# Longer transfer times, pinned first readers and a wider mark around solves in a hand-planned hybrid decoder layer

## The chip, the core and the metric

The kernel runs on one core of one Trainium2 chip. The metric is device microseconds (us) of one execution, taken as the median of several. TensorE (PE) multiplies matrices, with weight loads (PEld) running ahead of the matmuls; VectorE (DVE), ScalarE (ACT) and GpSimd (POOL) do the elementwise work; SyncE (SP) issues nearly all transfers (DMA). In this trace each engine, and the queue of SP, works through its instructions in the order of its program; one that has to wait holds those behind it.

## What is computed

One decoder layer on 2048 tokens of width 1024, all in float32. A normalised input is multiplied by one wide matrix whose columns feed three groups of heads and a gate. The parts that matter here:

```python
h = rms_norm(x, norm_in[l])
c_q, c_kv, k_rope, gdn_qkv, gdn_a, gdn_b, mem_q, gate = split_cols(h @ w_in[l], IN_SPLITS)
...
o_mla = causal_mla(q_nope, q_rope, k_nope, k_rope, v_mla).reshape(B, S, MLA_HEADS * MLA_V)
qkv = jax.nn.silu(causal_depthwise_conv(gdn_qkv, gdn_conv[l])).astype(jnp.float32)
...
L = jnp.where(strict, jnp.einsum('bhncd,bhnjd->bhncj', k_beta, k) * decay, 0.0)
T = lax.linalg.triangular_solve(L + eye, jnp.broadcast_to(eye, L.shape), left_side=True,
                                lower=True, unit_diagonal=True)
...
o_mem = memory_attention(mem_q..., mk..., mv...)
mixed = jnp.concatenate([o_mla, o_gdn, o_mem], axis=-1) * jax.nn.silu(gate)
x = x + mixed @ w_out[l]
return rms_norm(x, norm_final)
```

The second group of heads (gated delta rule, "GDN") needs a triangular solve for every chunk of tokens.

## The kernel before, in words

**Products in three parts.** Every large product is made of three matmuls on a high and a low part of each operand (`mm3`): high by high, high by low, low by high. So each weight tile `wr` that is loaded from HBM is split before use: `wh` is a rounded copy made on ACT or DVE, `wl` is the rest `wr - wh`, made on POOL or DVE. `lesser` (L618 to L620) picks the engine for `wl` (and for `bwl`, the same thing for the smaller weights `bw`): POOL, if the planner's clock of POOL isn't ahead of its clock of PE by more than a slack (500 ns for `wl`, 0 for `bwl`), else DVE.

**Two phases.** Phase 1 (up to about 1150 us; `phase[0] == 0`) streams the input projection: for each half of the tokens 34 column tiles, each in two units of 24 products (matmuls named `ip`). While these run, background generators do everything that hangs on their results: convolutions, the low-rank projections (`qb`, `kb`, `vb`), the memory keys and values (`mk`, `mv`, weights `bw`), and for each half and each of four heads one GDN chain (`delta_head`, eight chains in all). Phase 2 is attention (`sc`, `pt`, `av`) and the output projection (`op`).

**One GDN chain.** Row factors go out to memory and come back spread over all partitions (stores `rows_n`, `rows_g`, loads `fr`, `gr`). DVE scales keys and queries by them (`kq`), PE multiplies (`kk`), DVE writes the triangular systems `LT`; their diagonal blocks go out (`lsys`) and come back in another layout (`lt`). Then comes **the solve**: 62 small GpSimd instructions in a row that alternate between `pr` and `X` (L937 to L943). The result is stored (`tsys<-X`) and loaded into the tile `inv` (`inv0`, `inv1`); DVE transposes blocks of it (`mid<-inv`), PE finishes the inverse, and a scan over eight chunks follows (`pa`, `st`, `st_odd`), with loads of `gv` and `aT`.

**The order is planned by a model.** The Python program keeps a clock `T` for each engine and one for the transfers, with a cost for every instruction (`Timed`, L245 to L258). The clock of PE advances with the matmuls of the stream. A background generator is resumed when the clock of PE has reached the time at which, by the model, its last step is done (`pump`); at that moment its next instructions are written into the program. So the model's idea of when a transfer lands or a solve ends decides where the dependent instructions stand in the queues of DVE, ACT, POOL, PE and SP. For a transfer (`issue`, L292 to L303) the model takes 475 ns of SP, then

```python
        t = max(t + 650, T["DMA"]) + free(out) * out.shape[0] * 4 / 360
        T["DMA"] = t
        wrote(out, "SP", t + 700)
```

so the transfers run one after the other at 360 bytes per ns, and a reader on another engine sees the tile 900 ns after that (700 and 200). A transfer whose source isn't ready yet is kept in a list (`late`) with a similar estimate. For a solve the model takes 147 ns and 2.1 ns an element for each instruction, and about 100 ns between them.

**After the planner, a list scheduler.** The program so written passes through a scheduler that may move an instruction ahead of earlier ones of its engine where its own estimate says that it can start sooner; `tc.keep_in_program_order` forbids that for one instruction: it stays behind the instruction traced just before it on its engine. The stores `tsys<-X` and the loads of `inv` are already held that way (`behind=True`), as are transfers into `rows*` and `lsys*`.

Of the kernel before, what the change touches and what calls it, by code (L numbers as in the profile page):

```python
# [39 lines left out]
TRIG_AT = 1  # L40
MEM_AT = 44
STRICT = False
LONG = "012k3q", "0123qk"
CONV = 4
CBIAS = 2000.0
# [4 lines left out]
SLACK = {"wl": 500.0, "bwl": 0.0}  # L50
# [16 lines left out]
def hybrid_layer(ctx, tc, a, out):  # L67
    nc = tc.nc
    V, A, G, PE = nc.vector, nc.scalar, nc.gpsimd, nc.tensor
# [80 lines left out]
    PS = {"mm": 4, "g": 2, "scan": 2}  # L150
    rings = {t: [] for t in PS}
    in_psum = set()
    tiles = set()
    step_end = [0.0]
    tab = [None]

    def free(ap):
        return int(np.prod(ap.shape[1:]))
# [77 lines left out]
    pin = [False]  # L236
    phase = [0]

    def pinned(ins):

        if pin[0]:
            tc.keep_in_program_order(ins)
        return ins

    class Timed:  # L245
# [3 lines left out]
        def __getattr__(self, op):  # L249
            f = getattr(self.eng, op)  # L250

            def call(*args, **kw):
                out = kw["out"] if "out" in kw else args[0]
                outs = [out] + ([kw["accum_out"]] if "accum_out" in kw else [])
                ins = [x for x in (*args, *kw.values()) if hasattr(x, "tensor") and not any(x is o for o in outs)]
                note(self.name, self.cost(op, args, kw, out), outs, ins)
                return pinned(f(*args, **kw))  # L257
            return call  # L258

    V, A, G, PE = (Timed(nc.vector, "DVE", dve_cost), Timed(nc.scalar, "ACT", act_cost),  # L260
# [6 lines left out]
    def dma(out, in_, awaited=True, first=False, behind=False):  # L267
        touch(in_, out)
        t = max(arrival(in_, "SP"), used.get(out.tensor.name, 0.0), floor.get(out.tensor.name, 0.0))
        crowd = not first and T["PE"] > 0 and T["SP"] > T["PE"] + BACK  # L270
        if crowd or t > max(0.0, max(T["PE"], T["SP"]) + DEFER):
            if crowd:
                t = max(t, T["SP"] + 475 * sum(x[0] >= T["SP"] for x in late))
            late.append((t, out, in_, behind))
            t += 1125 + free(out) * out.shape[0] * 4 / 360
            wrote(out, "SP", t + 700)
            if awaited:
                step_end[0] = max(step_end[0], t + 900)
        else:
            issue(t, out, in_, behind, awaited)  # L280
# [9 lines left out]
        pinned(nc.gpsimd.dma_start(out=raw(out), in_=raw(in_)))  # L290

    def issue(t, out, in_, behind, awaited):  # L292
        t = max(T["SP"], T["PE"], t) + 475
        T["SP"] = t
        t = max(t + 650, T["DMA"]) + free(out) * out.shape[0] * 4 / 360
        T["DMA"] = t
        wrote(out, "SP", t + 700)
        used[in_.tensor.name] = max(used.get(in_.tensor.name, 0.0), t + 200)
        if awaited:
            step_end[0] = max(step_end[0], t + 900)  # L300
        ins = pinned(nc.sync.dma_start(out=raw(out), in_=raw(in_)))  # L301
        if (behind or out.tensor.name[:4] in ('rows','lsys')) and not pin[0]:
            tc.keep_in_program_order(ins)  # L303
# [313 lines left out]

    def lesser(name):  # L618

        return G if T["POOL"] <= T["PE"] + SLACK[name] else V  # L620

    class Job:

# [210 lines left out]
    def delta_head(hf, h, q, k, res):  # L834
# [102 lines left out]
        for j in range(31):  # L937
            n = j // 4 + 1
            w = 31 - j
            prv = pr[:, 0:n * w].rearrange("p (n w) -> p n w", w=w)  # L940
            G.tensor_tensor(prv, X[:, 0:n, j:j + 1].broadcast_to([P, n, w]),
                            lt[:, j, j + 1:32].unsqueeze(1).broadcast_to([P, n, w]), op=ALU.mult)
            G.tensor_tensor(X[:, 0:n, j + 1:32], X[:, 0:n, j + 1:32], prv, op=ALU.subtract)  # L943
        yield 0
        for cs in range(4):
            dma(out=tsys[hf][h].rearrange("s (n e) i -> e s n i", e=4)[cs], in_=X[cs * 32:(cs + 1) * 32],
# [1234 lines left out]
```

## Time and profile before

| what | value |
|---|---|
| median of 3 runs | 1859.41 us (1857.65 to 1865.71) |
| the profiled execution | 1856.66 us, span of its instructions 1854.9 us |
| PE busy | 1745.2 us, 94% of the span |
| DVE, ACT, POOL busy | 1203.0, 733.1, 510.2 us |
| mean granted TensorE clock | 0.978 of full |

Busy time counts the engine's own work; a waiting engine is idle. Nearly all instructions carry the line of the helper that records them (L257) and transfers that of `issue` (L301), so groups are told apart by their tiles: `out<-in`, buffer numbers left out. `PEclk` is the granted clock of TensorE, 1 being 2.4 GHz and 0.5 being 1.2 GHz; a value between them is a mean of stretches at either level. "SPq" is SP's queue of transfers.

### The profile page before, as it was taken

How to read it: one execution, taken by the hardware profiler on the slowest of the kernel's cores; microseconds unless marked ns; L12 is line 12 of the kernel's file. 1: busy time of each engine (PE TensorE's matmuls, PEld its weight loads, DVE VectorE, ACT ScalarE, POOL GpSimd, SP SyncE). 2: the span in 40 equal slices, each digit the busy share in tenths (PEclk: the TensorE clock that was granted, in tenths of full speed). 3: DMA queues.
4: the chain of work that ended last, by engine and by line, in shares of the span. 5: the costliest groups of instructions: out<-in, count | busy, mean ns of one | idle time of the engine just before them, and what ended most of it. 6: DMA issues, size and time to landing. Idle time of an engine off the chain costs nothing.

```text
span 1854.9 us, 28648 instructions
## 1 busy us (share of the span) xinstructions
PE 1745.2 (94%) x9780; PEld 1464.9 (79%) x9780; DVE 1203.0 (65%) x2696; ACT 733.1 (40%) x1792; POOL 510.2 (28%) x834
## 2 busy tenths in 40 slices
PE   6898799989998999899999799999999999899998
PEld 5676678877776888687888687889999998788886
DVE  8878586657776777546668263777776777543443
ACT  6354234334343445223454233455555556222221
POOL 5524615241161223342212524001111103511120
PEclk8899899999999999999999899999999999999999
DMA  5445347524647543455555367626252535754541
GB/s 191 156 127 153 118 154 219 183 82 136 213 131 242 160 158 121 151 195 165 181 190 192 99 208 225 183 89 185 73 173 70 157 105 176 228 168 157 184 150 61
DMA packets 242481, 292.49 MB, mean 158 GB/s; under 512 B 46848, under 2 KB 148224, under 8 KB 242336
## 3 DMA queue, kind: packets, MB, share of 16 engines
q1 hardware_dynamic: 239264, 282.28, 48.8%
q0 software_dynamic: 3072, 8.39, 1.3%
q8 instruction: 77, 1.26, 0.3%
q14 instruction: 68, 0.56, 0.1%
HBM read 197.53 MB, written 93.06 MB: 157 GB/s over the span
## 4 chain that ended last, share of the span: by engine, by line
PE 56%; DMA 6%; DVE 4%; POOL 3%; issue 2%; ACT 1%; SPq 1%; DVEq 0%; POOLq 0%; ACTq 0%
PE ip L257 14%; PE op L257 14%; PE sc L257 9%; PE av L257 6%; PE pt L257 4%; PE qb L257 2%; PE pa L257 2%; POOL X L257 1%; POOL pr L257 1%; SPq L301 1%; DMA wr<-in_w_in 1%; PE inv L257 1%; PE mv L257 1%; PE kk L257 1%; DVE y L257 1%
## 5 line engine op out<-in xcount | busy, mean ns | idle before, releaser
L257 PE MATMUL ip<-hh,wh 128*128 128x512 f32 x1088 | 457.2, 420 | 27.1 <-DVE elo L257 9.6
L257 PE MATMUL ip<-hh,wl 128*128 128x512 f32 x1088 | 433.0, 398 | 4.0 <-DVE wl L257 2.9
L257 PE MATMUL ip<-hl,wh 128*128 128x512 f32 x1088 | 432.1, 397 | 0.4 <-DVE hl L257 0.4
L257 PEld LDWEIGHTS ip<-hh,wh 128*128 128x128 f32 x1088 | 208.4, 192 | 64.5 <-DVE elo L257 10.0
L257 POOL TENSOR_TENSOR wl<-wr,wh 128x512 fp32r<-128x512 f32 x87 | 118.7, 1366 | 492.8 <-ACT wh L257 429.6
L257 PEld LDWEIGHTS ip<-hh,wl 128*128 128x128 f32 x1088 | 207.3, 191 | 50.4 <-DVE wl L257 3.6
L257 PEld LDWEIGHTS ip<-hl,wh 128*128 128x128 f32 x1088 | 208.8, 192 | 35.8 <-DVE hl L257 1.3
L257 PE MATMUL op<-wop,mh 128*128 128x512 f32 x480 | 151.2, 396 | 6.5 <-ACT mh L257 6.5
L257 ACT CAST wh<-wr 128x512 fp32r<-128x512 f32 x146 | 90.1, 618 | 157.8 <-PE ip L257 86.0
L257 DVE TENSOR_TENSOR tl<-pt,th 128x512 fp32r<-128x512 f32 (+2 forms) x208 | 119.8, 585 | 32.6 <-ACT th L257 30.3
L257 PE MATMUL sc<-kn,qn 128*128 128x512 f32 (+2 forms) x480 | 133.6, 380 | 0.0
L257 PE MATMUL av<-th,vn 128*128 128x256 f32 x576 | 130.3, 287 | 2.0 <-ACT th L257 2.0
L257 DVE SCALAR_TENSOR_TENSOR y<-raw,gdn_conv,y 128x512 f32<-128x512 f32 x144 | 125.4, 878 | 7.7 <-ACT y L257 6.3
L257 ACT CAST th<-pt 128x512 fp32r<-128x512 f32 (+2 forms) x158 | 80.1, 513 | 103.7 <-PE pt L257 96.5
L257 POOL TENSOR_TENSOR pr<-X,lt 128x60 f32<-128x60 f32 (+24 forms) x248 | 93.1, 376 | 97.6 <-DMA lt<-lsys 76.2
L257 PEld LDWEIGHTS op<-wop,mh 128*128 128x128 f32 x480 | 90.7, 190 | 27.0 <-ACT mh L257 7.0
L257 PEld LDWEIGHTS av<-th,vn 128*128 128x128 f32 x576 | 98.5, 189 | 6.9 <-ACT th L257 2.1
L257 POOL TENSOR_TENSOR X<-X,pr 128x60 f32<-128x60 f32 (+24 forms) x248 | 94.0, 379 | 19.4
L257 PE MATMUL sc<-kr,qr 128*128 128x512 f32 (+2 forms) x320 | 97.3, 381 | 0.0
L290 POOL DMA_DIRECT2D mix<-mo x64 | 34.8, 545 | 221.7 <-ACT mo L257 193.5
L257 PE MATMUL op<-wop,ml 128*128 128x512 f32 x240 | 94.5, 394 | 0.0
L257 POOL TENSOR_TENSOR og<-og,orow 128x512 f32<-128x512 f32 x32 | 45.9, 1451 | 172.5 <-DMA orow<-ri 130.4
(282 smaller groups left out, 3547.3 us busy)
## 6 DMA issues: line engine op xcount, KB each, us to landing
wr<-in_w_in SPq DMA_DIRECT2D x148, 256.0 KB, 2.9
fr<-rows_n SPq DMA_DIRECT2D x48, 256.0 KB, 4.4
mxo<-mix SPq DMA_DIRECT2D x16, 768.0 KB, 5.1
craw<-craw SPq DMA_DIRECT2D x40, 256.0 KB, 3.1
x<-in_xT SPq DMA_DIRECT2D x32, 256.0 KB, 5.3
gatem<-gt SPq DMA_DIRECT2D x32, 256.0 KB, 2.2
qn<-qn SPq DMA_DIRECT2D x32, 256.0 KB, 3.1
kn<-kn SPq DMA_DIRECT2D x32, 256.0 KB, 3.6
```

The source lines that it names most:

```text
L257: return pinned(f(*args, **kw))
L290: pinned(nc.gpsimd.dma_start(out=raw(out), in_=raw(in_)))
L301: ins = pinned(nc.sync.dma_start(out=raw(out), in_=raw(in_)))
```

## The change

In phase 1 (the expressions with `phase[0]` keep their old values in phase 2):

- the model's fixed time between SP and the data grows from 650 to 1500 ns, its rate falls from 360 to 200 bytes per ns, and the estimate for a transfer that isn't issued yet goes from 1125 ns and 360 to 2000 ns and 200;
- `issue` notes that a tile is being loaded (`landing`). The first recorded instruction that reads the tile as an input is then kept in program order, if the tile's name is in `LANDED`: `fr`, `gr`, `lt`, `inv0`, `inv1`, `X`, `tks`, `gv`, `aT`, `craw`, `gg`, `el`, `bw`. The weights of the stream (`wr`) and the input (`x`) aren't in it;
- a solve leaves a mark 8000 ns behind the planner's POOL clock at its end (`solving`), and until then `lesser` gives `wl` and `bwl` to DVE.

```diff
--- before.py
+++ after.py
@@ -40,6 +40,7 @@
 TRIG_AT = 1
 MEM_AT = 44
 STRICT = False
+LANDED = {"fr", "gr", "lt", "inv0", "inv1", "X", "tks", "gv", "aT", "craw", "gg", "el", "bw"}
 LONG = "012k3q", "0123qk"
 CONV = 4
 CBIAS = 2000.0
@@ -150,8 +151,10 @@
     PS = {"mm": 4, "g": 2, "scan": 2}
     rings = {t: [] for t in PS}
     in_psum = set()
+    landing = set()
     tiles = set()
     step_end = [0.0]
+    solving = [0.0]
     tab = [None]
 
     def free(ap):
@@ -253,8 +256,16 @@
                 out = kw["out"] if "out" in kw else args[0]
                 outs = [out] + ([kw["accum_out"]] if "accum_out" in kw else [])
                 ins = [x for x in (*args, *kw.values()) if hasattr(x, "tensor") and not any(x is o for o in outs)]
+                keep = False
+                for x in ins:
+                    if x.tensor.name in landing:
+                        landing.discard(x.tensor.name)
+                        keep = phase[0] == 0 and x.tensor.name.split("_")[0] in LANDED
                 note(self.name, self.cost(op, args, kw, out), outs, ins)
-                return pinned(f(*args, **kw))
+                r = f(*args, **kw)
+                if keep and not pin[0]:
+                    tc.keep_in_program_order(r)
+                return pinned(r)
             return call
 
     V, A, G, PE = (Timed(nc.vector, "DVE", dve_cost), Timed(nc.scalar, "ACT", act_cost),
@@ -272,7 +283,7 @@
             if crowd:
                 t = max(t, T["SP"] + 475 * sum(x[0] >= T["SP"] for x in late))
             late.append((t, out, in_, behind))
-            t += 1125 + free(out) * out.shape[0] * 4 / 360
+            t += (1125 if phase[0] else 2000) + free(out) * out.shape[0] * 4 / (360 if phase[0] else 200)
             wrote(out, "SP", t + 700)
             if awaited:
                 step_end[0] = max(step_end[0], t + 900)
@@ -290,9 +301,10 @@
         pinned(nc.gpsimd.dma_start(out=raw(out), in_=raw(in_)))
 
     def issue(t, out, in_, behind, awaited):
+        landing.add(out.tensor.name)
         t = max(T["SP"], T["PE"], t) + 475
         T["SP"] = t
-        t = max(t + 650, T["DMA"]) + free(out) * out.shape[0] * 4 / 360
+        t = max(t + (650 if phase[0] else 1500), T["DMA"]) + free(out) * out.shape[0] * 4 / (360 if phase[0] else 200)
         T["DMA"] = t
         wrote(out, "SP", t + 700)
         used[in_.tensor.name] = max(used.get(in_.tensor.name, 0.0), t + 200)
@@ -617,7 +629,7 @@
 
     def lesser(name):
 
-        return G if T["POOL"] <= T["PE"] + SLACK[name] else V
+        return G if max(T["POOL"], solving[0]) <= T["PE"] + SLACK[name] else V
 
     class Job:
 
@@ -941,6 +953,7 @@
             G.tensor_tensor(prv, X[:, 0:n, j:j + 1].broadcast_to([P, n, w]),
                             lt[:, j, j + 1:32].unsqueeze(1).broadcast_to([P, n, w]), op=ALU.mult)
             G.tensor_tensor(X[:, 0:n, j + 1:32], X[:, 0:n, j + 1:32], prv, op=ALU.subtract)
+        solving[0] = T["POOL"] + 8000
         yield 0
         for cs in range(4):
             dma(out=tsys[hf][h].rearrange("s (n e) i -> e s n i", e=4)[cs], in_=X[cs * 32:(cs + 1) * 32],
```

## Rows read from the trace of the kernel before

**Rows 1.** The page: PE's busy time, then the rate in 40 equal slices.

```profile
PE 1745.2 (94%) x9780; PEld 1464.9 (79%) x9780; DVE 1203.0 (65%) x2696; ACT 733.1 (40%) x1792; POOL 510.2 (28%) x834
...
GB/s 191 156 127 153 118 154 219 183 82 136 213 131 242 160 158 121 151 195 165 181 190 192 99 208 225 183 89 185 73 173 70 157 105 176 228 168 157 184 150 61
```

**Rows 2.** Busy time by stretch: from:to, length, each engine's us; PEclk, DMA share, GB/s.

```profile
50.00:1150.00 1100.00, 1025.17 (x5533) 840.62 (x5532) 738.87 (x1519) 414.27 (x1058) 373.03 (x634) 0.97 0.52 164
200.00:250.00 50.00, 41.22 (x243) 32.05 (x242) 28.94 (x57) 9.74 (x17) 18.06 (x36) 0.90 0.46 141
350.00:400.00 50.00, 43.63 (x223) 36.10 (x222) 32.18 (x68) 12.76 (x28) 28.21 (x66) 0.95 0.38 114
550.00:600.00 50.00, 45.20 (x276) 35.58 (x275) 35.33 (x57) 18.62 (x36) 8.26 (x7) 0.93 0.76 254
750.00:800.00 50.00, 44.17 (x263) 35.48 (x262) 22.40 (x40) 9.66 (x18) 10.97 (x25) 0.93 0.50 157
1000.00:1050.00 50.00, 40.38 (x206) 33.88 (x204) 23.60 (x45) 18.46 (x52) 25.30 (x65) 0.93 0.29 87
1050.00:1100.00 50.00, 47.96 (x353) 42.15 (x353) 34.19 (x69) 19.11 (x41) 15.10 (x13) 0.93 0.69 204
```

**Rows 3.** Waits of PE, 0 to 1190 us: total us, times, longest us.

```profile
PE pa L257 <- DVE st_odd L257: 10.9, 6, 6.4
PE kk L257 <- DVE kq L257: 10.7, 3, 6.7
PE ip L257 <- DVE elo L257: 9.6, 1, 9.6
```

**Rows 4.** Waits of the other engines, phase 1 (SP: up to 1190 us).

```profile
SPq L301 <- POOL wl L257: 136.4, 54, 9.8
...
SPq L301 <- POOL X L257: 38.8, 4, 14.6
...
DVE mid L257 <- DMA inv<-tsys: 10.4, 2, 6.4
...
POOL pr L257 <- DMA lt<-lsys: 76.2, 7, 17.7
```

**Rows 5.** Timeline around the end of the first solve: start us, us, instruction.

```profile
199.73 0.31 SPq L301 DMA_DIRECT2D rows_n<-rn  x1
...
214.53 1.28 POOL L257 TENSOR_TENSOR wl<-wr,wh 128x512 fp32r<-128x512 f32 x1
214.61 1.96 SPq L301 DMA_DIRECT2D tsys<-X  x3
...
220.61 0.69 DVE L257 TENSOR_TENSOR kq<-y,fr 128x512 f32<-128x512 f32 x1 [15.85 <-DMA fr<-rows_n]
```

**Rows 6.** Timeline around the end of the seventh solve, POOL and SP.

```profile
1042.84 1.26 POOL L257 TENSOR_TENSOR bwl<-bw,bwh 128x512 fp32r<-128x512 f32 x1
1047.99 1.27 POOL L257 TENSOR_TENSOR bwl<-bw,bwh 128x512 fp32r<-128x512 f32 x1 [3.89 <-ACT bwh L257]
...
1016.18 10.42 SPq L301 DMA_DIRECT2D wr<-in_w_in  x3
1044.13 0.33 SPq L301 DMA_DIRECT2D bw<-in_w_mk  x1
```

**Rows 7.** Busy time during solves five and eight; the sum of all eight.

```profile
725.30:758.50 33.20, 32.73 (x153) 26.68 (x152) 23.82 (x56) 16.16 (x49) 28.39 (x63) 1.00 0.30 94
...
1113.10:1136.20 23.10, 23.10 (x128) 18.98 (x128) 7.54 (x16) 5.03 (x15) 18.29 (x62) 1.00 0.81 245
sum 225.50, PE 218.01 PEld 180.08 DVE 132.84 ACT 81.83 POOL 187.12; mean PE 27.25 PEld 22.51 DVE 16.60 ACT 10.23 POOL 23.39
```

**Rows 8.** Transfers by tile: count, KB each, median us from issue to landing.

```profile
wr<-in_w_in SPq DMA_DIRECT2D x148, 256.0 KB, 2.9
fr<-rows_n SPq DMA_DIRECT2D x48, 256.0 KB, 4.4
```

**Rows 9.** The weight splits that DVE makes: busy us, mean ns, idle before.

```profile
L257 DVE TENSOR_TENSOR wl<-wr,wh 128x512 fp32r<-128x512 f32 x61 | 43.0, 706 | 20.4 <-ACT wh L257 20.0
```

## The prediction

> **What bounds the kernel now.** I read the slices and the busy times by stretch first, to find where PE isn't full; then the waits of PE and of the others; then the timeline around the worst places. In phase 1, from 50 to 1150 us, PE is busy for 1025.2 of 1100 us, so it stands still for 74.8 us, and its mean clock is 0.97 [rows 2]. The change touches phase 1 alone. Six stretches of 50 us hold half of the idle time: 200 to 250 (50 - 41.2 = 8.8 us), 350 to 400 (6.4), 550 to 600 (4.8), 750 to 800 (5.8), 1000 to 1100 (9.6 and 2.0), together 37.4 us [rows 2]. The other 16 stretches have 37.4 us as well, 2.3 each. The clock is low in the same six (0.90 to 0.95) [rows 2]: after PE has stood still, part of what follows runs at 1.2 GHz.
>
> The reader should see that all six follow the end of a solve. At the first, SP issues a store at 199.73 and then nothing until 214.61, when `tsys<-X` goes out: that store was at the head of the queue and waited 14.6 us for the solve. Behind it stood the `fr` loads, so DVE waited 15.85 us for `fr` [rows 5], and PE in turn up to 6.7 us for `kq` [rows 3]. At the seventh, SP finished an issue at 1016.18 + 10.42 = 1026.60 and took up the next at 1044.13, a load of `bw`: it waited 17.5 us, because the split `bwl` that reads the buffer had been given to POOL and stood behind the solve until 1042.84 [rows 6]; that is the 9.6 us wait of PE [rows 3]. A weight load that waits for a `wl` on POOL is the same thing, up to 9.8 us [rows 4]. After the third, DVE stood 6.4 us at `mid<-inv`, and PE 6.4 us for the `st_odd` behind it [rows 3, 4]. So the planner believes each solve to be over some 10 to 17 us before it is. Two reasons show: POOL waits 76.2 us for `lt` before seven solves, 10.9 each [rows 4], and a solve takes 225.5 / 8 = 28.2 us [rows 7], where the model's terms (62 instructions, 1560 elements to each half of them) give 62 x 0.147 + 3.3 x 2 + 62 x 0.1 = 22 us.
>
> **The transfer times.** For 256 KB the old model has the tile readable after 0.475 + 0.65 + 0.73 + 0.9 = 2.75 us, the new one after 0.475 + 1.5 + 1.31 + 0.9 = 4.2 us. The trace has 4.4 for `fr` and 2.9 for `wr` [rows 8]: the new figure is right for the loads of a GDN chain and 1.3 us too slow for the weights. The Trainium skill ("DMA: Bandwidth & Descriptors", section "Anatomy of one DMA — SWDGE (gpsimd) path") puts one transfer at about 2.0 us and its bytes over 436 GB/s, for the GpSimd path; an estimate from it for 256 KB is 2.6 us, which agrees with `wr` and not with `fr`. By that rule the new model is too slow everywhere, and the change would go the way of the slower rival below. What the time adds between `lsys` and the planned end of a solve: the store 0.85 + 0.07, the first load 0.85, and five loads of 128 KB in a row at 0.66 in place of 0.36 (1.5), together 3.2 us, and more when the model's queue is full. Of a wait of 14.6 us for `tsys` about 11 remain. So SP's 38.8 us for `X` [rows 4] shrink by 3 x 3.2 = 10 us and don't vanish; a second step, `tsys` to `inv`, is set 2 us later too.
>
> **The splits.** Starting at a solve's end or within 8 us of it, 12 splits stand on POOL, from 214.53 to 1047.99 [rows 5, 6]. They go to DVE, for 12 x 0.71 = 8.5 us of its time [rows 9]. DVE is busy for 22.4 to 35.3 of 50 us in the six stretches [rows 2], so that lies beside its idle time; were DVE full there, the splits would hold PE for the same 8.5 us. They no longer stand behind the solve, and neither do the loads that reuse their buffers.
>
> A price may come with it: a solve with 23.8 us of DVE work beside it took 33.2 us, one with 7.5 us took 23.1 [rows 7], so 0.62 us more for each us of DVE work. If half of the 8.5 us fell beside solves, they would grow by 2.6 us in all: I put 1 us on the path, with 0 and 2.6 as ends. The Trainium skill ("SBUF — State Buffer", section "Who interferes with whom") says that a VectorE instruction with two SBUF inputs and a GpSimd one that reads SBUF block each other; a split is such an instruction, and rows 7 agree with it. By that rule the whole 8.5 us could land on POOL: 8.5 in place of 1 in the sum.
>
> **The pins.** They add no instruction and no wait. A pinned reader can't be put ahead of what was traced just before it, so DVE's work ahead of `kq` and `mid` goes first. What is queued behind a pinned reader waits as it did. Cost: a solve pinned behind a split waits for ACT's `wh`; nobody waits for a solve sooner than `tsys`, so I put it at nothing. Without that cover it would be some 3.9 us for each, as POOL waited for ACT there [rows 6]. Two names do little: `gr` and `gg` are first read by instructions that write them in place, and those aren't seen as readers.
>
> **The sum**, in idle time of PE. Stretch 1000 to 1100: the `bwl` cause is gone, 10 of 11.6 us. 750 to 800: the split is gone and the `mid` wait is shorter, 4 of 5.8. 200 to 250: `fr` is still behind `tsys`, but less long, 4 of 8.8. 350 to 400: `mid` is later and pinned, 4.5 of 6.4. 550 to 600: 3 of 4.8. The two smaller `kq` waits, 10.7 - 6.7 = 4.0 us [rows 3]: 3. Together 28.5 us, from 0 to 41.4. The clock: (1 - clock) x 50 over the six rows is 21.5 us at most [rows 2]; part of the slow time falls where PE stands still anyway, so I take two thirds, 14.3, and of that the share that the idle time in the six loses (25.5 of 37.4), 9.8 us. Gains 38.3 us.
>
> Against it: every order in phase 1 is drawn anew, and new waits arise where there were none. No row shows them. From below it is 0; from above the 16 quiet stretches double their 37.4 us [rows 2]. I take 12, since most of the new times are nearer to the trace, and 1 for the longer solves. Net 38.3 - 13 = 25.3 us. The profiled execution took 1856.7 us, 1.8 more than its span, and stands 2.7 under the median: 1856.7 - 25.3 + 2.7 = 1834 us.
>
> **The rivals.**
> 1. *The new model is too slow.* Five slices of phase 1, each 46.4 us, moved 219, 213, 242, 208 and 225 GB/s [rows 1], more than the model's 200. There its queue falls behind by (107 / 200) x 46.4 = 25 us in all. Weights and inputs then seem late, the model's PE waits while the real one doesn't, and background instructions are written too early, ahead of matmuls that could run. It decides when the added waits exceed the 38 us gained. If the 25 us come back as waits, with the 14 us of clock that go with them as in the six stretches, and the 13 us above, the cost is 52: 1859.4 + 52 - 38 = 1873 us. For it: 2.9 us for `wr`. Against: weights are loaded two units ahead, so 1.3 us each are mostly hidden.
> 2. *The jam moves, and stays.* `tsys` is still queued some 11 us too early, and only the `bwl` and `kq` terms come: 10 + 3 + 4 of clock, less 13, so 1855 us: no change. For it: the model's cost of a solve isn't touched (22 against 28.2 us). Against: what lies behind `tsys` is also traced later.
> 3. *The pins do nothing*, because the list scheduler left those readers in place anyway. Without the 4.5 and 3 us and their 2 us of clock: 1844 us, still faster.
> 4. *All six stretches vanish* and little comes in their place: 41.4 + 14.3 gained, 5 lost, so 1809 us.
>
> **How the numbers follow.** Forecast (1820 to 1850) 0.43; rival 4 0.08; rival 3 0.13; rival 2 0.16; rival 1 0.20. A measurement of this kernel can tell about 0.5% from no change, 9.3 us, so faster means under 1850.1. Forecast, 3 and 4 are faster, 0.64; rival 2 is the same, 0.17 with its edges; slower 0.19. The predicted time is 1834 us. The range runs from 1807, just under rival 4, to 1872, just short of rival 1's middle: one in ten is left out at either side.
>
> **What would show it.** Right: SP's wait for `X` falls from 38.8 us to under 30; no `wl` or `bwl` starts on POOL within some us of a solve's end; DVE makes some 12 splits more; the `kq` waits of PE fall below 4 us; the rows of 1000 to 1100 lose their idle time. Wrong: new waits of PE over 4 us away from solves, mostly for DVE or ACT (rival 1); `tsys` again 10 us and more at the head of SP's queue with PE standing still (rival 2); or phase 1 shorter by 25 us but attention waiting at its start for a GDN chain that ends later, which none of the terms holds.

## The result: slower by 2.9%

| kernel | median of 5 runs | range | ratio |
|---|---|---|---|
| before | 1860.34 us | 1857.65 to 1865.71 | 1 |
| after | 1914.88 us | 1913.21 to 1920.16 | 1.0294 (95%: 1.0272 to 1.0316) |

Forecast were 1834 us and a range that ended at 1872: wrong in sign, and out of the range. The pins turn out to be free and the mark nearly so (0.8% alone); the whole loss comes with the longer transfer times in the model, and most of it with the model's one queue.

The profiled execution has a span of 1911.4 us, 56.5 more than before. The page's busy times of after:

```profile
PE 1773.3 (93%) x9780; PEld 1483.8 (78%) x9780; DVE 1210.2 (63%) x2706; ACT 731.7 (38%) x1789; POOL 503.9 (26%) x827
```

Beside [rows 1]: the same 9780 matmuls took 28.1 us more (1773.3 - 1745.2), and PE stood still for 138.1 us, 28.4 more than before (1911.4 - 1773.3 against 1854.9 - 1745.2). So half of the loss is waiting, and half is longer busy time. Most of that second half is the lower clock: set against PE's busy time, the clock record of the two traces has PE busy at 1.2 GHz for 94.2 us in place of 49.9, and half of the difference, 22.1 of the 28.1 us, is the time added (the mean granted clock is 0.963, before 0.978). The other 6 us were not traced to a cause. The busy time by stretch shows where the waiting lies, columns as in [rows 2]. After:

```profile
50.00:1150.00 1100.00, 1017.59 (x5368) 833.41 (x5366) 725.35 (x1482) 401.00 (x1011) 345.64 (x565) 0.96 0.50 157
200.00:250.00 50.00, 49.18 (x251) 40.28 (x250) 39.75 (x88) 15.85 (x32) 26.81 (x65) 1.00 0.48 137
350.00:400.00 50.00, 50.00 (x279) 42.95 (x277) 24.76 (x51) 13.00 (x37) 21.81 (x62) 1.00 0.52 158
550.00:600.00 50.00, 25.09 (x165) 19.45 (x164) 23.82 (x56) 11.47 (x27) 16.61 (x39) 0.69 0.43 133
750.00:800.00 50.00, 50.00 (x232) 41.26 (x231) 36.30 (x81) 24.07 (x65) 24.06 (x45) 1.00 0.45 137
1000.00:1050.00 50.00, 46.28 (x267) 39.62 (x267) 31.63 (x71) 20.87 (x56) 4.90 (x4) 1.00 0.67 217
1050.00:1100.00 50.00, 50.00 (x241) 41.64 (x240) 39.35 (x86) 25.65 (x70) 23.91 (x38) 1.00 0.43 130
...
1137.50:1261.50 124.00, 105.16 (x743) 87.77 (x741) 66.08 (x201) 40.84 (x122) 29.06 (x79) 0.91 0.59 180
```

The last stretch of it in the kernel before, which the rows ahead of the prediction don't hold:

```profile
1137.50:1261.50 124.00, 121.54 (x856) 106.42 (x856) 83.65 (x266) 56.94 (x152) 12.62 (x29) 1.00 0.53 157
```

Five of the six bad stretches are healed: 8.0, 6.4, 5.8, 5.9 and 2.0 us less idle time than in [rows 2], 28.1 in all, and the clock there is full. But two new holes are larger. At 550 to 600, the switch between the halves of the tokens, PE lost 20.1 us more and its clock fell to 0.69. From 1137.5 to 1261.5, the start of attention, it lost 16.4 us more at a clock of 0.91. Gains and holes together leave 20.0 of the 28.4 us: 8.1 of them lie just ahead of the second hole, from 1100 to 1137.5, 5.0 before 200 us, and the rest is scattered.

The first hole from near by (timeline: start, length, instruction, idle time before it and what released it): ACT, then POOL at the end of the fourth solve, then PE.

```profile
547.63 0.61 ACT L265 CAST wh<-wr 128x512 fp32r<-128x512 f32 x1
...
563.44 0.20 POOL L265 TENSOR_TENSOR pr<-X,lt 128x8 f32<-128x8 f32 x1
563.60 1.26 POOL L265 TENSOR_TENSOR wl<-wr,wh 128x512 fp32r<-128x512 f32 x1
564.82 0.21 POOL L265 TENSOR_TENSOR X<-X,pr 128x8 f32<-128x8 f32 x1
...
564.92 0.79 PE L265 MATMUL ip<-hh,wl 128*128 128x512 f32 x1 [12.29 <-POOL wl L265]
565.51 0.63 PE L265 MATMUL ip<-hh,wh 128*128 128x512 f32 x1
...
569.35 0.40 PE L265 MATMUL ip<-hh,wh 128*128 128x512 f32 x1
```

A split whose input was ready at 547.63 + 0.61 = 548.24 stands behind 61 of the 62 solve instructions, and the stream waits 12.3 us for it. The mark that should prevent this is set when the planner traces the solve. Either it had run out, by the planner's clock, when this split was traced, or the split was traced ahead of the solve; the record doesn't show which.

The second hole is seen in the end of the stream and the start of the last solve. The last product before; then, of after, the last product, the start of the last solve on POOL, and the two longest entries of PE's waits from 1137.5 to 1262 us (total, times, longest):

```profile
1162.16 0.39 PE L257 MATMUL ip<-hh,wl 128*128 128x512 f32 x1
...
1137.54 0.40 PE L265 MATMUL ip<-hh,wl 128*128 128x512 f32 x1
...
1179.13 0.24 POOL L265 TENSOR_TENSOR pr<-X,lt 128x31 f32<-128x31 f32 x1 [3.77 <-DMA lt<-lsys]
...
PE mv L265 <- ACT bwh L265: 3.6, 3, 2.2
PE inv L265 <- DVE mid L265: 3.0, 3, 1.3
```

The stream is done 24.6 us sooner than before, but the last solve begins 66 us later (before 1113.1). What a chain does after its solve, `inv`, `pa`, `st`, now runs with no product left to fill PE: 10.0 us of PE's waits in this stretch are for links of the chains. Another 6.4 us are for the splits of the memory weights (`mv` and `mk` for `bwh` and `bwl`), which run behind the stream too. Before, the last solve began 49 us ahead of the last product; now it begins 42 us behind it.

### The profile page after: what moved, and what is told of

It reads as the page before. It is cut to its first block, busy times and chain, and to the rows that moved or that the text cites. A ratio compares the mean times of both kernels' runs of the same rounds, so it can differ in the third digit from the quotient of the medians.

```text
span 1911.4 us, 28633 instructions
## 1 busy us (share of the span) xinstructions
PE 1773.3 (93%) x9780; PEld 1483.8 (78%) x9780; DVE 1210.2 (63%) x2706; ACT 731.7 (38%) x1789; POOL 503.9 (26%) x827
## 5 line engine op out<-in xcount | busy, mean ns | idle before, releaser
L265 PE MATMUL ip<-hh,wl 128*128 128x512 f32 x1088 | 434.0, 399 | 17.1 <-POOL wl L265 12.3
L265 POOL TENSOR_TENSOR wl<-wr,wh 128x512 fp32r<-128x512 f32 x79 | 109.0, 1379 | 533.8 <-ACT wh L265 416.9
L265 PE MATMUL sc<-kn,qn 128*128 128x512 f32 (+2 forms) x480 | 138.1, 388 | 3.2 <-ACT me L265 1.6
L265 DVE SCALAR_TENSOR_TENSOR y<-raw,gdn_conv,y 128x512 f32<-128x512 f32 x144 | 117.5, 818 | 10.2 <-ACT y L265 8.8
L265 PEld LDWEIGHTS op<-wop,mh 128*128 128x128 f32 x480 | 90.8, 191 | 24.6 <-ACT mh L265 4.2
L265 POOL TENSOR_TENSOR X<-X,pr 128x60 f32<-128x60 f32 (+24 forms) x248 | 99.8, 402 | 19.3
```

Source lines behind the costliest of these rows:

```text
L265: r = f(*args, **kw)
```

## The experiments

Edits are against the kernel before, unless the text says otherwise. "Left" is how many products `ip` of the half (of 1632) were still to be done when its last solve, the fourth and the eighth, began; it is read from the busy time of the tile `ip` from 0 to that moment (rows stand in the fourth set). "Behind" is the start of the eighth solve less that of the last product, in us.

| kernel | median, us | ratio to before (95%) | left, half 1 and 2 | behind |
|---|---|---|---|---|
| before | 1860.3 | 1 | 168, 144 | -49 |
| after | 1914.9 | 1.0294 (1.0272 to 1.0316) | 43, 0 | 42 |
| null | 1855.8 | 1.0003 (0.9991 to 1.0015) | as before | as before |
| pins_only | 1855.4 | 1.0002 (0.9993 to 1.0012) | 171, 145 | -50 |
| mark_only | 1869.5 | 1.0078 (1.0057 to 1.0100) | 156, 183 | -66 |
| trans_only | 1908.1 | 1.0297 (1.0263 to 1.0332) | 0, 0 | 43 |
| fixed_only | 1877.4 | 1.0103 (1.0084 to 1.0121) | 175, 24 | -20 |
| rate_only | 1936.4 | 1.0421 (1.0398 to 1.0445) | 32, 0 | 24 |
| trans_h0 | 1885.8 | 1.0142 (1.0124 to 1.0161) | 0, 102 | -46 |
| trans_h1 | 1890.9 | 1.0157 (1.0114 to 1.0200) | 169, 0 | 50 |
| slow_stream | 1914.5 | 1.0303 (1.0262 to 1.0343) | 93, 138 | -53 |
| slow_chain | 1923.0 | 1.0340 (1.0312 to 1.0367) | 27, 0 | 39 |
| after_split | 1918.9 | 1.0325 (1.0297 to 1.0354) | 43, 0 | 41 |
| after_mem | 1915.5 | 1.0305 (1.0278 to 1.0332) | 43, 0 | 34 |
| queue_only | 1908.6 | 1.0258 (1.0239 to 1.0278) | 45, 0 | 55 |
| no_queue | 1887.0 | 1.0132 (1.0115 to 1.0150) | 49, 0 | 15 |
| resume_late | 1856.6 | 0.9977 (0.9963 to 0.9990) | 182, 132 | -50 |
| short | 1907.3 | 1.0245 (1.0227 to 1.0262) | 181, 202 | -68 |
| rl_pins_mark | 1860.0 | 1.0021 (1.0012 to 1.0031) | 146, 72 | -23 |
| rl_pins_bwl | 1860.6 | 1.0023 (1.0010 to 1.0036) | 171, 84 | -31 |

The kernel before ran anew beside each set, at medians from 1855.8 to 1861.8 us; the ratios go by those.

### First set: the parts alone

**trans_only**: the longer times, without pins and mark.

```diff
-            t += 1125 + free(out) * out.shape[0] * 4 / 360
+            t += (1125 if phase[0] else 2000) + free(out) * out.shape[0] * 4 / (360 if phase[0] else 200)
...
-        t = max(t + 650, T["DMA"]) + free(out) * out.shape[0] * 4 / 360
+        t = max(t + (650 if phase[0] else 1500), T["DMA"]) + free(out) * out.shape[0] * 4 / (360 if phase[0] else 200)
```

> The kernel before with the longer transfer times alone; no pins, no mark. Theory A (the model is now too slow, its PE clock waits for loads that have long landed, so background work is written ahead of matmuls that could run): this alone carries the loss, 1905 to 1930 us, with PE idle again around the half switch (550 to 600 us of the kernel after) and at the start of attention. Theory B (the pins hold readers behind slow neighbours, or the mark loads DVE): under 1875 us.

Measured 1908.1 us: the whole loss. It also has most of the gain: the five healed stretches held 47.95, 50.00, 47.85, 47.45 and 46.68 us of PE, 22.6 of the 28.1 us, with no mark and no pin. SP's wait for `X` in it (up to 1260 us; [rows 4] have 38.8):

```profile
SPq L301 <- POOL X L257: 14.5, 4, 11.9
```

So with the longer times alone the jam at `tsys` did shrink, by more than the 10 us forecast. How much of the gain is that, and how much that the order was drawn anew and the solves fell elsewhere, this run doesn't separate.

**pins_only**: `LANDED`, `landing` and `keep` alone.

```diff
+                if keep and not pin[0]:
+                    tc.keep_in_program_order(r)
```

> The kernel before with the pins alone (same planner clocks as before). Theory A: 1845 to 1870 us, since no planned time moves. Theory B: over 1880 us, the pins being the cause.

Measured 1855.4 us, no difference. The pins move instructions and give nothing: the `kk<-kq` waits that they should have shortened are 17.2 us, the longest 13.2, before 10.7 and 6.7 [rows 3].

**mark_only**: `solving` alone.

```diff
-        return G if T["POOL"] <= T["PE"] + SLACK[name] else V
+        return G if max(T["POOL"], solving[0]) <= T["PE"] + SLACK[name] else V
...
+        solving[0] = T["POOL"] + 8000
```

> The kernel before with the mark after solves alone. The prediction gave it 10 us for the memory weights at 1000 to 1100 us and 4 us at 750 to 800, with some 5 us of clock: 1835 to 1845 us if these terms hold and nothing new arises. Theory B: over 1870 us, DVE being too full for the 12 splits.

Measured 1869.5 us, 0.8% slower, between the two theories. Busy time by stretch, mark_only:

```profile
750.00:800.00 50.00, 49.38 (x304) 39.98 (x303) 28.34 (x59) 20.51 (x59) 20.30 (x44) 1.00 0.48 157
1000.00:1050.00 50.00, 48.71 (x322) 41.55 (x321) 35.69 (x69) 24.88 (x66) 29.82 (x66) 1.00 0.47 145
...
1150.00:1200.00 50.00, 40.64 (x279) 33.66 (x277) 21.67 (x75) 13.03 (x33) 5.20 (x11) 0.83 0.71 200
```

Two of the gains that the prediction gave to the splits came, 5.2 and 8.3 us. Only in part for its reason: seven splits still start on POOL at a solve's end or within 8 us of it (before 12), one of them right behind the seventh solve:

```profile
1033.00 1.30 POOL L265 TENSOR_TENSOR bwl<-bw,bwh 128x512 fp32r<-128x512 f32 x1
```

SP no longer waits for it (17.5 us before [rows 6]). With six more splits on DVE (four `wl`, two `bwl`) the planner's clocks differ, and so does the order behind them: at 1150 to 1200 PE was busy for 49.44 us before and is for 40.64 now, of which 8.4 us are waits for `mid`. The last of the four `tsys` stores that it hangs on went out at 1153.86 us, 15.6 us after the first, since other transfers had come between them in SP's queue. So what was gained in two stretches was given back where the new order happens to be worse.

**null**: 660 ns for 650 in the old model.

> The kernel before with the model's fixed time of an issue at 660 in place of 650 ns: a change of no meaning, which shows what a redrawn order alone can do. Theory A: within 8 us of 1859 us. Theory C (every redrawn order costs or gains tens of us by chance, so that no cause is to be found in the change): off by over 15 us either way.

Measured 1855.8 us, ratio 1.0003. The order didn't change at all, so this shows the noise of the measurement, and not, as meant, what a redrawn order can do by chance.

### Second set: which term, and which half

**rate_only** has only 200 for 360 bytes per ns; **fixed_only** only 1500 for 650 ns and 2000 for 1125.

> The kernel before with the model's rate of 200 bytes per ns in phase 1 alone; the fixed times stay 650 and 1125 ns. Theory A1 (the queue of the model, at 200, falls behind a chip that moves 205 to 254 GB/s in the busy stretches, and that is what carries the loss): 1885 to 1915 us. Theory A2 (it is the longer fixed time, which stretches each of the ten or so transfers of a GDN chain): under 1870 us.

> The kernel before with the longer fixed times (1500 and 2000 ns) in phase 1 alone; the rate stays 360. Theory A1: 1845 to 1870 us. Theory A2: 1880 to 1910 us, with the last solve of the GDN chains starting after the input projection has ended, as in the kernel after (1179 against 1137 us).

Measured 1936.4 and 1877.4 us: the rate alone loses 4.2%, more than both together, the fixed time 1.0%. Both lie outside what either theory expected. SP's wait for `X` in rate_only (up to 1260 us) and the busy time of phase 1:

```profile
SPq L301 <- POOL X L257: 90.8, 8, 20.6
...
50.00:1150.00 1100.00, 999.47 (x5241) 812.41 (x5240) 711.55 (x1453) 398.14 (x1005) 368.38 (x572) 0.96 0.47 152
```

So rate_only loses twice. Its last chain is late, as in trans_only, and the jam at `tsys` has grown to 90.8 us, where fixed_only has 27.5 and trans_only 14.5. From 50 to 1150 us PE is busy for 25.7 us less than before, in trans_only for 9.7 less.

**trans_h0** and **trans_h1** have the long times in the first or the second half of the tokens only, by a flag `half[0]` that is set where the second half's jobs begin (trans_h0, the changed line of `issue`; the estimate changes likewise).

```diff
...
-        t = max(t + 650, T["DMA"]) + free(out) * out.shape[0] * 4 / 360
+        t = max(t + (1500 if phase[0] == 0 and half[0] == 0 else 650), T["DMA"]) + free(out) * out.shape[0] * 4 / (200 if phase[0] == 0 and half[0] == 0 else 360)
...
```

> The longer transfer times only while the first half of the tokens is streamed. If the half switch (550 to 600 us, 25 us of standing still and the low clock) and the end of phase 1 are two losses of their own, this has the first and not the second: 1875 to 1895 us, PE idle at 550 to 600 us, and attention starting as in the kernel before. If the loss at the end only follows from the delay at the switch, this carries nearly all: over 1900 us.

> The longer transfer times only while the second half is streamed. Two losses of their own: 1880 to 1905 us, no standing still at 550 to 600 us, and PE idle for some 25 us with a low clock in the 150 us after the projection's end, because the last GDN chains end late. If the end only follows from the switch: under 1870 us.

Measured 1885.8 and 1890.9 us, 1.4% and 1.6%: the two add up to the 3.0% of trans_only. (The profiled execution of trans_h1 was its quickest, 1876 us.) Each makes its own hole; of the other's, trans_h0 has a part (4.2 us at 1150 to 1200), trans_h1 nothing. First trans_h0, then trans_h1:

```profile
550.00:600.00 50.00, 26.64 (x97) 20.72 (x98) 28.25 (x59) 16.11 (x39) 28.05 (x66) 0.69 0.50 153
1150.00:1200.00 50.00, 45.29 (x295) 36.40 (x294) 23.50 (x82) 14.62 (x49) 12.75 (x39) 0.90 0.70 206
```

```profile
550.00:600.00 50.00, 45.04 (x271) 35.37 (x270) 30.41 (x51) 17.03 (x33) 9.22 (x7) 0.90 0.72 244
1150.00:1200.00 50.00, 38.89 (x270) 33.15 (x268) 24.02 (x88) 16.77 (x49) 19.57 (x60) 0.86 0.65 192
```

So most of the loss sits at the end of a half, in both. At that place the last chain of the half ends, and its cover, the half's stream, runs out.

### Third set: whose transfers, and two single waits

**slow_stream** has the long times for `wr`, `x` and `wp` alone, **slow_chain** for all others.

```diff
...
+        t = max(t + (1500 if phase[0] == 0 and out.tensor.name.split("_")[0] in ("wr", "x", "wp") else 650), T["DMA"]) + ...
...
```

> The kernel before with the longer transfer times for the loads of the projection stream alone (wr, x, wp). Whole of both (trans_only) cost 53 us. Theory S (the model's TensorE is held up by its own stream loads, falls behind the real one, and splits land in the middle of solves): most of the loss is here, 1885 to 1910 us, with a TensorE wait of about 10 us for a POOL wl inside a solve between 500 and 600 us. Theory C (the readers of the chain's small loads are put too late, and the background is thinned out for them): nearly nothing here, 1850 to 1870 us.

> The kernel before with the longer transfer times for every load and store but those of the projection stream. Theory S: nearly nothing, 1850 to 1870 us. Theory C: most of the 53 us, 1885 to 1910 us, with the last read of the projection stream earlier than in the kernel before (1162 us) and the loss after 1050 us. If each makes one of the two losses that the halves showed, both come out near 1880 us, the one with the loss at 550 to 600 us, the other with that at 1050 to 1300 us.

Measured 1914.5 and 1923.0 us. Neither theory expected both: each half of the transfers loses the whole. They lose in different ways. slow_chain has the two holes of after, with 27 and 0 products left. slow_stream keeps 93 and 138 products left, and loses inside the stream. Its largest wait, on PE and on ACT:

```profile
580.47 0.80 PE L257 MATMUL ip<-hh,wh 128*128 128x512 f32 x1 [18.59 <-ACT wh L257]
...
579.80 0.62 ACT L257 CAST wh<-wr 128x512 fp32r<-128x512 f32 x1 [18.73 <-DMA wr<-in_w_in]
```

That `wr` was issued at 574.26, behind a `tsys` store that SP could not issue before 569.47: the jam of [rows 5] again, at another solve. SP's whole wait for `X` (up to 1260 us) has grown from 38.8 us:

```profile
SPq L301 <- POOL X L257: 59.7, 7, 19.6
```

My reading is that the model's stream is late here, so the planner's time runs on while few products are done, and `tsys` is written too early against its solve. The jam is shown; that this is its reason is not, and the fourth and the eighth solve themselves begin with fewer products left than before.

**after_split**: the kernel after, with the split of 563.60 forced to DVE.

```diff
-        return G if max(T["POOL"], solving[0]) <= T["PE"] + SLACK[name] else V
+        hurry = phase[0] == 0 and 600e3 < T["PE"] < 610e3
+        return G if max(T["POOL"], solving[0]) <= T["PE"] + SLACK[name] and not hurry else V
```

> The kernel after, with the one split that stands inside solve 4 (TensorE waits 12.5 us for it at 552 us) put on VectorE. If that wait is the loss of the half switch: 550 to 600 us rises from 25.1 us of TensorE busy to about 40, and the kernel takes 1895 to 1903 us. If the solve that it waited beside is what is late, other waits for inv and rb take its place (they stand at 574 to 597 us): 1908 us or more.

Measured 1918.9 us: nothing won. POOL, PE and the stretch:

```profile
566.82 2.50 POOL L265 TENSOR_TENSOR wl<-wr,wh 128x512 fp32r<-128x512 f32 x2
...
568.14 0.80 PE L265 MATMUL ip<-hh,wl 128*128 128x512 f32 x1 [7.73 <-POOL wl L265]
...
550.00:600.00 50.00, 26.21 (x169) 20.16 (x167) 26.60 (x58) 13.41 (x36) 19.24 (x43) 0.69 0.45 142
```

The stream now waits 7.7 us for the next split, which stands behind the solve, and the stretch holds 26.2 in place of 25.1 us. The longest wait of the hole was a symptom.

**after_mem**: the kernel after, with `MEM_AT` 37 for 44.

> The kernel after with the projections of the memory chunk started 7 steps earlier in its order (MEM_AT 37 for 44). If attention waits at its start for these (mkp and mvp are loaded at 1211 us, before 1115 us): 1880 to 1900 us. If it waits for the GDN chain of the last heads (last solve ends at 1203 us, before 1136 us), unchanged, 1910 to 1920 us, or slower, since the projections then take their place in a stretch that was full.

Measured 1915.5 us, unchanged. The `mk` products begin at 950 in place of 1095 us and the second hole stays: from 1137.5 to 1261.5 PE is busy for 94.8 us, in after for 105.2. The loads of `mkp` stayed at 1211 us, and here PE waits for one:

```profile
1217.37 0.58 PE L265 MATMUL sc<-mkp,qn 128*128 128x256 f32 x1 [8.96 <-DMA mkp<-mk]
```

That load stood in SP's queue behind the `tsys` stores of the last solve, for which SP had issued nothing from 1192.24 to 1207.24. In after no wait of PE for `mkp` shows. So here too it was the late solve that attention waited for, by way of another tile.

### Fourth set: the model's queue

By [rows 2] the chip moved 164 GB/s on average from 50 to 1150 us, and 254 in one stretch. The model sends its transfers one after the other: at 360 bytes per ns the average fills 164 / 360 = 46% of its queue, at 200 it fills 82%, and the stretch of 254 doesn't fit. In a queue that full, a chain's load waits for weights in front of it, by the model; in the trace `fr` took 4.4 us from issue to landing and `wr` 2.9 [rows 8].

**queue_only**: each transfer takes its old time, but holds the queue at 200. **no_queue**: each takes the new time, but holds the queue at 360.

```diff
-        t = max(t + 650, T["DMA"]) + free(out) * out.shape[0] * 4 / 360
-        T["DMA"] = t
+        b_ = max(t + 650, T["DMA"])
+        t = b_ + free(out) * out.shape[0] * 4 / 360
+        T["DMA"] = b_ + free(out) * out.shape[0] * 4 / (360 if phase[0] else 200)
```

```diff
+        b_ = max(t + (650 if phase[0] else 1500), T["DMA"])
+        t = b_ + free(out) * out.shape[0] * 4 / (360 if phase[0] else 200)
+        T["DMA"] = b_ + free(out) * out.shape[0] * 4 / 360
```

> The kernel before, each transfer taking its old time (650 ns and 360 bytes per ns), but occupying the model's one queue of transfers at 200 bytes per ns, so that only those behind it are later. Theory Q (the model's transfers run one after the other; at 200 bytes per ns that queue is nearly full, and the loads of the chains wait in it): nearly all of the loss of the rate alone (4.2%), 1900 to 1940 us, with the fourth and the eighth solve beginning when about 1584 and 3264 products of the stream are done (before 1464 and 3120). Theory L (each transfer's own longer time delays the chain that waits for it): 1850 to 1870 us.

> The kernel before with the new fixed times and each transfer's own duration at 200 bytes per ns, but occupying the model's queue at 360 bytes per ns as before. Theory Q: the loss falls from 3.0% to little more than the fixed times alone cost (1.0%): 1870 to 1890 us. Theory L: 1900 us or more.

Measured 1908.6 and 1887.0 us: the queue alone loses 2.6%, and without it the new times lose 1.3%. In queue_only the two solves begin at 1587 and 3264 products, which theory Q had put at 1584 and 3264. (1.3% is a little more than the fixed times' 1.0%, and queue_only loses less than the rate's 4.2%; so a part stays with the transfers' own times.)

**resume_late**: the old times, but a generator that issued a transfer is resumed 1450 ns later, as much as the longer times add to 256 KB by themselves.

```diff
-            step_end[0] = max(step_end[0], t + 900)
+            step_end[0] = max(step_end[0], t + 900 + (0 if phase[0] else 1450))
...
```

> The kernel before with its transfer times, but a background generator that has issued a transfer is resumed 1450 ns later (what the longer times add for 256 KB without a queue). If any later resuming loses the time: 1880 to 1910 us. If the time is lost only where the last chain of a half has no products of the stream left beside it (theory Q's second part): 1850 to 1870 us, the eighth solve beginning with some 120 products left.

Measured 1856.6 us, 0.9977: no loss, if anything 0.2% won. Resuming later isn't what loses. The counts show the difference: busy time of the tile `ip` up to the start of the fourth and the eighth solve, first before, then after, queue_only and resume_late (the first count in a row is PE's):

```profile
0.00:511.50 511.50, 381.17 (x1464) 274.30 (x1465) 40.00 (x59) 0.00 (x0) 0.96 0.50 158
0.00:1113.10 1113.10, 806.62 (x3120) 576.98 (x3120) 63.30 (x93) 50.20 (x85) 0.97 0.52 164
```

```profile
0.00:533.10 533.10, 408.31 (x1589) 298.41 (x1589) 44.10 (x65) 0.00 (x0) 0.96 0.50 154
0.00:1179.10 1179.10, 834.49 (x3264) 607.50 (x3264) 67.82 (x100) 54.25 (x92) 0.96 0.51 160
```

```profile
0.00:517.00 517.00, 402.06 (x1587) 294.24 (x1588) 44.85 (x66) 0.00 (x0) 0.97 0.50 159
0.00:1196.80 1196.80, 835.82 (x3264) 605.09 (x3264) 68.12 (x100) 54.41 (x92) 0.96 0.52 161
```

```profile
0.00:497.90 497.90, 377.49 (x1450) 271.16 (x1451) 40.64 (x60) 0.00 (x0) 0.97 0.51 160
0.00:1106.20 1106.20, 811.04 (x3132) 582.51 (x3133) 63.84 (x94) 51.02 (x86) 0.97 0.52 164
```

3264 is the whole stream: in after and queue_only nothing of it was left for the last chain. resume_late has 132 products left, before 144.

**short**: the opposite change, 400 ns and 500 bytes per ns (875 in the estimate).

> The kernel before with shorter transfer times in the model's first phase (400 ns and 500 bytes per ns for 650 and 360; 875 for 1125 in the estimate). By theory Q the chains come earlier, their ends keep more of the stream beside them, and nothing is lost there: 1845 to 1865 us. If instructions written too early are as dear as ones written too late, waits of TensorE for fr, inv and gv loads appear in the middle of the stream: 1875 us or more.

Measured 1907.3 us: the other direction loses nearly as much. There is no hole at the end of the halves (181 and 202 products left), but in the stream PE is busy for 992.3 us from 50 to 1150, 32.9 less than before. Its longest wait of PE, 14.6 us, with what led to it, on POOL, SP, ACT, DVE and PE:

```profile
301.03 1.26 POOL L257 TENSOR_TENSOR wl<-wr,wh 128x512 fp32r<-128x512 f32 x1
...
303.40 0.54 SPq L301 DMA_DIRECT2D bw<-in_w_vb  x1
...
307.35 0.62 ACT L257 CAST bwh<-bw 128x512 fp32r<-128x512 f32 x1 [15.25 <-DMA bw<-in_w_vb]
...
308.00 0.69 DVE L257 TENSOR_TENSOR bwl<-bw,bwh 128x512 fp32r<-128x512 f32 x1 [15.55 <-ACT bwh L257]
...
310.21 0.58 PE L257 MATMUL pa<-r,inv 128*128 128x128 f32 x1 [14.62 <-DVE r L257]
```

A chain of five queues: a split behind a solve on POOL, the weight load that waits for its buffer at the head of SP's queue (SP issued nothing from 284.5 to 302.3), a `bw` load behind that, ACT, and DVE, where the `r` that PE needs stands behind a `bwl`. SP's waits for `X` grow from 38.8 [rows 4] to 55.7 us. It is what the prediction read in [rows 5, 6], only more of it: by my reading because with shorter times everything is written further ahead of its data.

**rl_pins_mark** and **rl_pins_bwl**: the pins and the mark on resume_late; in the second the mark holds for `bwl` alone.

> The kernel after with its pins and its mark, but the old transfer times and a background generator resumed 1450 ns later after a transfer: the change with its extra wait taken out of the model's queue. By theory Q the chains stay in place (last solve with about 90 products left) and the time is that of the mark alone or less, 1850 to 1872 us; if the pins and the mark are of use once readers are written later, below 1850 us; if the longer transfer times weren't what loses, 1900 us.

> The same, but the mark after a solve holds for the split bwl alone (wl goes to POOL as in the kernel before). The one jam at a bw load after the seventh solve (9.6 us of idle TensorE in the kernel before) would go, and the order stays near that of resume_late (1856.6 us): 1845 to 1856 us. If redrawing the order gives back what the jam cost, 1855 to 1870 us.

Measured 1860.0 and 1860.6 us, 1.002: the change without its queue loses nothing that counts, and gains nothing. No kernel here beats the one before by more than 0.3%.

## Why the prediction was wrong, point by point

**The failed step** is "Against it": 12 us for new waits, "since most of the new times are nearer to the trace". The profiled execution came out 56.5 us longer after all that was gained. With the 28.1 us of idle time that the healed stretches gave back, the new waits and the clock that went with them cost 84.6 us or more, where the sum had 12. Three things were wrong in that term.

*What was priced.* I compared the time of one transfer with the trace (4.2 and 2.75 us against 4.4 and 2.9). The change also alters how long a transfer blocks all later ones, since the model has one queue. The same number, 200, stood for both. Rival 1 saw the queue, but only in the five slices over 200 GB/s; at 82% mean filling the chain's loads wait in the model nearly everywhere. queue_only shows what that costs: 2.6% with every transfer's own time as it was.

*The bound.* It went by the quiet stretches of phase 1, 37.4 us at most, as though a wait could come only where a small one was. The second hole lies behind 1137.5 us, outside the window of the sum. The prediction's last sentence named it, "attention waiting at its start for a GDN chain that ends later, which none of the terms holds", and gave it neither a price nor a chance. One row more was needed for it: [rows 7] has the last solve end at 1136.2 us, and the last product began at 1162.16, so the last chain's cover was some 26 us thick.

*The direction.* Rival 1 had the sign, and 1873 us. It thought that background would be "written too early"; in after the last chain is too late against the stream, which ends 24.6 us sooner while the solve begins 66 us later. Stores written ahead of their solves are what short and slow_stream show, and that costs 2.4 and 3.0%. The argument against rival 1, that weights loaded two units ahead hide the extra time, fell with slow_stream, where the stream's loads alone are longer.

**What held.** The idle time that would go: 22.5 us forecast for the five healed stretches, 28.1 measured. That the sums agree is partly luck: trans_only has 22.6 of it without mark and pins, to which the sum gave a large part, and mark_only took 5.2 and 8.3 us off 750 to 800 and 1000 to 1050 with splits still behind both solves. The pins cost nothing; and as rival 3 had it, they bring nothing, though instructions did move. `mid<-inv` waits fell, as forecast.

**What didn't.** The rows of after that answer to [rows 3, 4, 9] (waits of SP and PE up to 1260 us, of DVE and POOL; then DVE's splits):

```profile
SPq L313 <- POOL X L265: 39.3, 3, 15.8
...
PE kk L265 <- DVE kq L265: 13.2, 2, 13.0
...
DVE mid L265 <- DMA inv<-tsys: 2.6, 2, 1.9
...
POOL pr L265 <- DMA lt<-lsys: 60.4, 6, 23.8
...
L265 DVE TENSOR_TENSOR wl<-wr,wh 128x512 fp32r<-128x512 f32 x69 | 49.6, 719 | 24.4 <-ACT wh L265 24.1
```

SP's wait for `X` was to fall under 30 us and is 39.3, so the jam stays, as rival 2 had it. Its reason, that a solve's cost in the model wasn't touched, doesn't suffice: with the longer times alone the wait fell to 14.5. What brings it back beside pins and mark is open. The `kq` waits were to fall under 4 us and are 13.2. Eight splits went to DVE, not twelve; one stands inside a solve (563.60), and nine more start on POOL at a solve's end or within 8 us of it. The prediction could have seen this: it read that the planner believes a solve to be over 10 to 17 us too early, and a mark of 8 us behind that moment runs out before the solve does.

**The price of DVE work beside solves.** Eight solves took 230.6 us with 151.55 us of DVE work beside them; [rows 7] have 225.5 with 132.84. That is 5.1 us for 18.7, or 0.27 each, less than the 0.62 of the two solves there. Neither is shown to be a price, since a solve that lasts longer has more DVE work beside it by its length alone. The Trainium skill ("SBUF — State Buffer", "Who interferes with whom") has a VectorE instruction with two SBUF inputs contend with GpSimd's reads; the direction agrees with the trace, and nothing near the whole of DVE's time landed on POOL.

**The rule on transfers.** By the estimate from the Trainium skill ("DMA: Bandwidth & Descriptors", "Anatomy of one DMA — SWDGE (gpsimd) path"), 2.6 us for 256 KB on the GpSimd path, the new times are too long, and the change would have gone the way of the slower rival. It did go slower, by that rule for a part at most: the page is of one transfer's time, and no_queue, which has the new times without the queue, lost 1.3% of the 2.9.

**What stays open.** The products left tell whether a half's end has a hole, not how large: no_queue and queue_only have nearly the same counts (49, 0 and 45, 0) and lose 1.3 and 2.6%; in the first the last solve begins 15 us behind the stream, in the second 55, but rate_only with 24 us loses 4.2%. SP's wait for `X` doesn't simply follow the times either: 14.5 us in trans_only, but 56.9 in no_queue, which has the same times without the queue. The null kernel drew no new order, so chance was not measured as meant; pins_only, resume_late and the two kernels made from it did draw new ones and lie between -0.2 and 0.2%, which speaks against a loss of 2.9% by mere redrawing. mark_only has 0.8%, so of the differences under 1% here none is explained with certainty. One rival stands untested: the old constants may have been set by trial to where this kernel's order comes out well, so that any larger move of them, in either direction, loses somewhere.

## What to carry to other kernels

In a planner that writes the order, a transfer's latency and the rate of its queue are two numbers, to be changed apart: check the second against the bytes per second that the profile shows, since here a serial queue filled to 82% cost 2.6% by itself. Times nearer to the trace are no gain in themselves: neither longer nor shorter ones made this kernel faster. When a dependent chain is hidden behind a stream, count what is left of the stream where the last chain starts, before and after; the end of each such stretch, and what begins behind it, belongs into the sum. And take the longest wait of a hole away alone before believing it: here the next one took its place.

## What was not expected of the hardware

The clock costs nearly as much as the waiting: some 22 us of longer busy time at 1.2 GHz beside 28.4 us of idle time. In the timeline above, the matmul after the wait of 12.3 us took 0.79 us and the next 0.63, and at 569.35, 4.4 us later, one took 0.40 us; the granted clock of the stretch is 0.69, a mean of the two levels, 1.2 and 2.4 GHz.
